# Start offsets of split weight buffers, modulo 256 bytes, in a two-layer decoder trunk

## The chip, the cores and the metric

The kernel runs on one core of a Trainium2 chip. The metric is the device time of one execution in microseconds (us). The engines are named as in the profile: PE is TensorE, with PEld its weight load, DVE is VectorE, ACT is ScalarE, POOL is GpSimd and SP is SyncE.

## The reference

Two layers over 256 tokens of width 1024, in float32. Cut to what matters here, which is the matrix products:

```python
for l in range(2):
    h = rms_norm(x, norm_mix_pre[l])
    q, k, v, lru_x, lru_gate, glu_in, gate_logits = split(h @ w_in[l])      # 1024 x 11776
    y_a = dilated_attention(q, k, v) @ w_o_attn[l]                          # 512 x 1024
    y_b = rg_lru(lru_x, lru_gate, lru_wa, lru_wx, ...) @ w_o_lru[l]         # 1024 x 1024
    y_c = conformer_conv(glu_in, ...) @ w_o_conv[l]                         # 1024 x 1024
    merged = sum_i sigmoid(gate_logits_i) * y_i
    x = x + rms_norm(merged @ w_out[l], norm_mix_post[l])                   # 1024 x 1024
    h = rms_norm(x, norm_mlp_pre[l])
    u = square(relu(h @ w_mlp_up[l]))                                       # 1024 x 4096
    x = x + rms_norm(u @ w_mlp_down[l], norm_mlp_post[l])                   # 4096 x 1024
```

## The kernel before

The host cuts all weights of a layer into 92 chunks of 128 partitions x 2048 float32 (1 MB each) and puts them in the order in which they are used (`chunk_plan`, `ORDER`). The kernel streams them in that order. The function `weights` does for one chunk: a DMA on SP into one of two `raw` buffers; a cast on ACT (line 416, in halves of 1024) that writes the high part `whi` in type float32r; a subtraction on DVE (line 429) that writes the low part `wlo`, which is raw minus high. The activations are split in the same way (`hh` and `hl`, `uh` and `ul`, and so on), and a product is three matmuls on PE (line 476): high by high, low by high, high by low.

There are two kinds of chunk.

- A **stationary** chunk (kinds `ws`, `rope` and `oa` in the plan: all of lx, lg, glu, q, k, ga, gb, gc, oa, ob, oc, and up but its first two chunks, which are ua). The weights are loaded into the array, 128 columns at a time, and 256 columns of activations stream past. `ws_items` sets the order of its 48 matmuls: two halves, and in each half first 16 matmuls with the high part (for each of 8 slices: with `hh`, then with `hl`), then 8 matmuls with the low part. In the trace such a half is 16 rows `whi_...` and one row `wlo_... x8`.
- A **moving** chunk (kind `as`: v, wo, ua and dn). Here the activations are loaded and 512 columns of weights stream past, 24 matmuls in one chunk. `as_items` sets the order: in each of two groups of 12, high and low part in turn for eight matmuls, then four with the high part.

All matmuls with weights follow each other on PE in the order of the plan (`main` chains them); a list scheduler with a cost model (`Sched.run`), which knows nothing of addresses, sets the rest. In the attention part (from the chunk q11 of a layer to its gc3) PE also does scores (`sc`), transposes (`tp`) and products with values (`pv`), which stand between the matmuls of the chunks, at the ends of the 16-row pieces above all. In the MLP each pair of up chunks is followed by a pair of dn chunks.

The addresses are what this case is about. `whi` and `wlo` have three buffers each (`NHI`), and the chunks take them in turn. A buffer has 2048 + 32 float32, which is 8320 bytes a partition, or 32 and a half times 256. So neighbouring buffers differ by 128 bytes modulo 256. In the built program the high buffers start at 128, 0 and 128 bytes modulo 256, the low buffers at 0, 128 and 0. Inside a buffer, a class `Shifted` begins the data 64 bytes (16 float32) late for stationary chunks and for v1 and v2, and at 0 for the other moving chunks. Data therefore stand like this, where "192/64" says that the high part begins 192 bytes and the low part 64 bytes past a multiple of 256:

| chunk | two chunks of three | every third chunk |
|---|---|---|
| stationary, and v1, v2 | 192/64 | 64/192 |
| v0, wo, ua, dn | 128/0 | 0/128 |

All slices inside a chunk are multiples of 256 bytes, so every matmul of a chunk has the offset of its part. The activations of the matmuls (`hh`, `hl`, `uh`, `ul`, the slots) all start 128 bytes past a multiple of 256. One chunk is an exception: the second dn chunk of the seventh group in layer 0 (`dn61`, "held") is split into eight slots, and there both parts stand at 128/128; its matmuls for the first 128 tokens and those for the second 128 tokens are run at two places.

The chunks of the MLP by their standing, in the order of time in layer 0: up4, up5 at 192/64; up6 at 192/64, up7 at 64/192; up8 at 64/192, up9 at 192/64; up10, up11 at 192/64, and so on with this period of three pairs. The dn pairs between them stand at 0/128 then 128/0; both at 128/0; 128/0 then 0/128; and so on.

Of the kernel before, what the change touches and what calls it, by code (L numbers as in the profile page):

```python
# [8 lines left out]
F32R = mybir.dt.float32r  # L9
# [4 lines left out]
P = 128  # L14
# [5 lines left out]
CHUNK = 2048  # L20
# [26 lines left out]
def chunk_plan():  # L47
    q0, k0, v0, lx0, lg0, gl0, br0 = 0, 1536, 3072, 4608, 5632, 6656, 8704
    plan = []

    def ws(name, mat, c0, c1=None):
        plan.append((name, "ws", mat, (c0, c0 + P if c1 is None else c1)))

    for n in ORDER:
        kind, a = n[:2], n[2:]
        if n[0] == "v":
            for kb in range(2):
                plan.append((f"{n}{kb}", "as", "w_in", (kb, v0 + int(n[1]) * 512)))
        elif n[0] in "qk":
            plan.append((n, "rope", "w_in", (q0 if n[0] == "q" else k0) + int(n[1]) * 512 + int(n[2]) * 256))  # L60
        elif kind == "gl":
            ws(n, "w_in", gl0 + int(n[3]) * P, gl0 + D + int(n[3]) * P)
        elif kind == "oa":
            plan.append((n, "oa", "w_o_attn", int(a) * 512))
        elif kind != "lw":
            mat, c0 = {"lx": ("w_in", lx0), "lg": ("w_in", lg0), "ga": ("w_in", br0), "gb": ("w_in", br0 + D),
                       "gc": ("w_in", br0 + 2 * D), "ob": ("w_o_lru", 0), "oc": ("w_o_conv", 0)}[kind]
            ws(n, mat, c0 + int(a) * 256)
    for c in range(2):
        for kb in range(2):  # L70
            plan.append((f"wo{c}{kb}", "as", "w_out", (kb, c * 512)))
    for kb in range(9):
        if kb == 0:
            plan += [(f"ua{k}", "as", "w_mlp_up", (k, 0)) for k in range(2)]
        elif kb < 8:
            ws(f"up{2 * kb}", "w_mlp_up", (2 * kb) * 256)
            ws(f"up{2 * kb + 1}", "w_mlp_up", (2 * kb + 1) * 256)
        if kb > 0:
            for c in range(2):
                plan.append((f"dn{kb - 1}{c}", "as", "w_mlp_down", (kb - 1, c * 512)))  # L80
    return plan
# [11 lines left out]
NHI = 3  # L93
# [10 lines left out]
LINE = 128  # L104
# [272 lines left out]
def trunk_kernel(ctx: ExitStack, tc: tile.TileContext, x_d, pos_d, w_d, lruw_d, par_d, gain_d, const_d, id_d, out_d):  # L377
    nc = tc.nc
    cp = ctx.enter_context(tc.tile_pool(name="cp", bufs=1))
    wp = ctx.enter_context(tc.tile_pool(name="wp", bufs=1))  # L380
    sp = ctx.enter_context(tc.tile_pool(name="sp", bufs=1))
    pp = ctx.enter_context(tc.tile_pool(name="pp", bufs=1, space=bass.MemoryType.PSUM))
    S = Sched()
# [4 lines left out]
    def slot(name, dt=F32, shape=(P, 2, T)):  # L388
        return S.buf(sp, shape, dt, "s2", name, NSLOT)
# [58 lines left out]
    def dma(eng, out, in_, nbytes):  # L448
        def fn():
            o = out.ap() if isinstance(out, View) else out  # L450
            i = in_.ap() if isinstance(in_, View) else in_
            eng.dma_start(out=o, in_=i)

        e = {id(nc.gpsimd): "POOL", id(nc.scalar): "ACT"}.get(id(eng), "SP")
        o = S.op(e, DMA_ISSUE[e], fn, views(in_), views(out))
        o.dma = nbytes / DMA_RATE / 1e3
        return o
# [40 lines left out]
    def split(hi, lo, src, scale=None):  # L498
        if scale is None:
            return act(hi, src, AF.Copy), tt(lo, src, hi.f32(), OP.subtract)  # L500
        return (act(hi, src, AF.Copy, scale=scale),
                stt(lo, src, scale, hi.f32(), OP.mult, OP.subtract))

    KIND = {p[0]: p[1] for p in chunk_plan()}
# [3 lines left out]
    def weights(l, name, spread=False):  # L508
        c = CIDX[name]
        assert c == used[l], (name, c, used[l])  # L510
        used[l] += 1
        nm = f"{name}_{l}"
        raw = S.buf(wp, (P, CHUNK), F32, "raw", f"raw_{nm}", NRAW)
        if l or c:
            o = dma(nc.sync, raw.all(), w_d[l * NCH + c], CHUNK * P * 4)
            if l == 0 and c in late:
                S.follow(o, late[c])
        else:
            for s in range(2):
                o = dma(nc.sync, raw[:, s * HALF:(s + 1) * HALF], w_d[0][:, s * HALF:(s + 1) * HALF], HALF * P * 4)  # L520
                if ORDER[0][0] == "v":
                    S.follow(o, x1_load)
        if spread:
            hs, ls = [], []
            for q in range(4):
                hs.append(slot(f"whi_{nm}{q}", F32R, (P, 512)))
                ls.append(slot(f"wlo_{nm}{q}", F32R, (P, 512)))
                for o in split(hs[q].all(), ls[q].all(), raw[:, q * 512:(q + 1) * 512]):
                    o.prep = True
            return [(Quarters(hs[2 * s:2 * s + 2]), Quarters(ls[2 * s:2 * s + 2])) for s in range(2)]  # L530
        off = 0 if KIND[name] == "as" and name[:2] not in ("v1", "v2") else LINE // 8
        hi = Shifted(S.buf(wp, (P, CHUNK + LINE // 4), F32R, "whi", f"whi_{nm}", NHI), off)
        lo = Shifted(S.buf(wp, (P, CHUNK + LINE // 4), F32R, "wlo", f"wlo_{nm}", NHI), off)
        n = HALF if l == 0 and c < 2 else PREP
        for b in range(0, CHUNK, n):
            for o in split(hi[:, b:b + n], lo[:, b:b + n], raw[:, b:b + n]):
                o.prep = True
        return [(Part(hi, s * HALF), Part(lo, s * HALF)) for s in range(2)]
# [201 lines left out]
    for l in range(L):  # L740
# [49 lines left out]
        def glu(i):  # L790
            w = weights(l, f"glu{i}")
            ps = mm_ps(f"glu{i}_{l}")
            gemm(f"glu{i}", w, ps, hr)
            if i % 2 == 0:
                upad[i // 2] = S.buf(sp, (P, 2, 288), F32, "upad", f"upad{i}_{l}", 4)
                memset(upad[i // 2][:, :, 0:30], 0.0)
            u2 = upad[i // 2]
            th = slot(f"gth{i}_{l}", shape=(P, T))
            act(th.all(), ps[:, 1, :], AF.Tanh, scale=0.5)
            stt(u2[:, i % 2, 30:30 + T], th.all(), 1.0, ps[:, 0, :], OP.add, OP.mult)  # L800
            if i % 2 == 1:
                conv_pair(i // 2)
# [3 lines left out]
        def lx(j):  # L806
            w = weights(l, f"lx{j}")
            ps = mm_ps(f"lx{j}_{l}")
            gemm(f"lx{j}", w, ps, hr)
            xp = S.buf(sp, (P, 2, 260), F32, "xp", f"xp{j}_{l}", 2)  # L810
            memset(xp[:, :, 0:3], 0.0)
            act(xp[:, :, 3:3 + T], ps.all(), AF.Copy)
            u = slot(f"lu{j}_{l}")
            for s in range(2):
                i = 2 * j + s
                act(u[:, s, :], ps[:, s, :], AF.Identity, scale=p1(par, CW + 24 + i), bias=p1(par, CB + i))
            for k in range(3):
                for s in range(2):
                    i = 2 * j + s
                    stt(u[:, s, :], xp[:, s, k:k + T], p1(par, CW + k * 8 + i), u[:, s, :], OP.mult, OP.add)  # L820
            lu[j] = u
            luh[j] = slot(f"luh{j}_{l}", F32R)
            lul[j] = slot(f"lul{j}_{l}", F32R)
            split(luh[j].all(), lul[j].all(), u.all())
# [3 lines left out]
        def lg(j):  # L828
            w = weights(l, f"lg{j}")
            ps = mm_ps(f"lg{j}_{l}")  # L830
            gemm(f"lg{j}", w, ps, hr)
            q = slot(f"gq{j}_{l}")
            act(q.all(), ps.all(), AF.Square, scale=0.044715 ** 0.5)
            stt(q.all(), q.all(), 1.0, ps.all(), OP.add, OP.mult)
            act(q.all(), q.all(), AF.Tanh, scale=0.7978845608028654)
            g = slot(f"gel{j}_{l}")
            stt(g.all(), q.all(), 1.0, ps.all(), OP.add, OP.mult)
            gel[j] = g
# [319 lines left out]
        for t in range(2):  # L1158
            nm = f"pm{l}{t}"
# [82 lines left out]
        for t in range(2):  # L1242
            nm = f"pd{l}{t}"
# [100 lines left out]
```

## Time and profile before

| | |
|---|---|
| median of 3 runs | 1123.68 us (1123.16 to 1127.1) |
| the profiled execution | 1124.8 us, of which its span is 1123.0 us |
| granted TensorE clock, mean | 0.998 |
| PE busy | 1103.7 us, 98% of the span |
| DVE busy | 903.7 us, 80% |
| ACT busy | 726.0 us, 65% |
| chain that ended last | PE 82%, DVE 9%, DMA 4%, ACT 3% |

The span is the time from the first to the last instruction. Busy times of matmuls overlap: a matmul of 256 columns is shown with 276 to 283 ns, while the next one starts 113 or 118 ns later. How fast PE really goes is therefore read from the starts of rows, or from the chain of work that ended last, where a piece of so many matmuls has a length without overlap.

### The profile page before, as it was taken

What the parts mean: (1) busy time and instruction counts of PE and PEld (TensorE: products, weight loads), DVE (VectorE), ACT (ScalarE), POOL (GpSimd) and SP (SyncE); (2) the same over time, 40 slices, a digit from 0 to 9 for tenths busy, and PEclk for the clock granted to TensorE, in tenths of its full rate; (3) what the DMA queues carried; (4) which work ended last, traced back from release to release, by engine and by line L of the source; (5) the groups of instructions that cost most, each with busy time, mean ns of one, the idle gap of its engine ahead of it and who ended that gap; (6) DMA issues with size and microseconds to landing.
All of it is one profiled execution on the core that took longest, in us unless ns stands there. A gap on an engine that the chain in (4) does not pass through costs nothing.

```text
span 1123.0 us, 20583 instructions
## 1 busy us (share of the span) xinstructions
PE 1103.7 (98%) x8258; PEld 1027.6 (92%) x8258; DVE 903.7 (80%) x1380; ACT 726.0 (65%) x1184; POOL 70.8 (6%) x156
## 2 busy tenths in 40 slices
PE   7999998999999999999999999999999999999997
PEld 6999998999999889988889999989989998988996
DVE  6999999999969875555679999999997789655554
ACT  5879938588765554444569897469766656444443
POOL 1000021111000010000000000221200001000000
PEclk9999999999999999999999999999999999999999
DMA  8654365655255555555556553765634365655551
GB/s 293 245 208 151 146 219 205 215 165 174 99 186 188 214 199 189 208 193 182 201 188 205 190 179 121 255 216 170 214 124 151 117 240 185 212 192 185 190 203 52
DMA packets 37649, 209.76 MB, mean 187 GB/s; under 512 B 6449, under 2 KB 9777, under 8 KB 14130
## 3 DMA queue, kind: packets, MB, share of 16 engines
q1 hardware_dynamic: 32976, 200.05, 50.7%
q0 software_dynamic: 4576, 8.40, 2.2%
q8 instruction: 65, 1.06, 0.4%
q14 instruction: 30, 0.25, 0.1%
q10 hardware_dynamic: 2, 0.00, 0.0%
HBM read 201.08 MB, written 1.05 MB: 180 GB/s over the span
## 4 chain that ended last, share of the span: by engine, by line
PE 82%; DVE 9%; DMA 4%; ACT 3%; issue 1%; SPq 1%; DVEq 0%; POOL 0%; ACTq 0%
PE dn L476 15%; PE up L476 14%; PE glu L476 8%; PE v L476 5%; PE gc L476 4%; PE wo L476 4%; PE lx L476 4%; PE oc L476 4%; PE lg L476 4%; PE k L476 3%; PE ga L476 3%; PE ob L476 2%; PE ua L476 2%; PE oa L476 2%; PE gb L476 1%; DMA qk<-r1q 1%
## 5 line engine op out<-in xcount | busy, mean ns | idle before, releaser
L429 DVE TENSOR_TENSOR wlo_dn<-raw_dn,whi_dn 128x1024 fp32r<-128x1024 f32 (+1 forms) x66 | 75.8, 1190 | 68.4 <-ACT whi_dn L416 68.4
L416 ACT CAST whi_dn<-raw_dn 128x1024 fp32r<-128x1024 f32 (+1 forms) x66 | 64.4, 1022 | 75.6 <-PE dn L476 44.0
L433 DVE SCALAR_TENSOR_TENSOR c<-upad,parh,c 128x256 f32<-128x256 f32 x256 | 110.5, 479 | 0.1
L476 PE MATMUL up<-hh_mlp,whi_up 128*128 128x256 f32 x448 | 106.3, 278 | 0.0
L476 PE MATMUL up<-hl_mlp,whi_up 128*128 128x256 f32 x448 | 106.0, 278 | 0.0
L476 PE MATMUL dn<-wlo_dn,uh 128*128 128x512 f32 x256 | 100.5, 393 | 0.0
L476 PE MATMUL dn<-whi_dn,uh 128*128 128x512 f32 x256 | 100.4, 392 | 0.0
L429 DVE TENSOR_TENSOR wlo_up<-raw_up,whi_up 128x1024 fp32r<-128x1024 f32 x56 | 66.4, 1222 | 39.1 <-ACT whi_up L416 39.1
L423 ACT ACTIVATE cpd<-upad,parh 128x256 f32<-128x256 f32 x224 | 94.6, 500 | 4.1 <-DVE c L429 4.1
L476 PEld LDWEIGHTS up<-hl_mlp,whi_up 128*128 128x128 f32 x448 | 84.3, 188 | 0.6
L476 PEld LDWEIGHTS up<-hh_mlp,whi_up 128*128 128x128 f32 x448 | 84.2, 188 | 0.6
L416 ACT CAST whi_up<-raw_up 128x1024 fp32r<-128x1024 f32 x56 | 56.2, 1048 | 36.4 <-PE dn L476 17.4
L476 PE MATMUL dn<-whi_dn,ul 128*128 128x512 f32 x256 | 70.8, 392 | 0.0
L429 DVE TENSOR_TENSOR cpd<-cpd 128x1024 f32<-128x1024 f32 (+2 forms) x84 | 63.5, 775 | 0.9 <-ACT cpd L423 0.9
L476 PE MATMUL up<-hh_mlp,wlo_up 128*128 128x256 f32 x448 | 60.7, 278 | 0.0
L476 PE MATMUL glu<-hl_mix,whi_glu 128*128 128x256 f32 x256 | 59.6, 276 | 0.0
L476 PE MATMUL glu<-hh_mix,whi_glu 128*128 128x256 f32 x256 | 59.6, 276 | 0.0
L476 PEld LDWEIGHTS dn<-whi_dn,ul 128*128 128x128 f32 x256 | 48.0, 188 | 10.8
L476 PEld LDWEIGHTS dn<-wlo_dn,uh 128*128 128x128 f32 x256 | 48.0, 188 | 10.3
L476 PEld LDWEIGHTS dn<-whi_dn,uh 128*128 128x128 f32 x256 | 48.1, 188 | 10.3
L476 PEld LDWEIGHTS up<-hh_mlp,wlo_up 128*128 128x128 f32 x448 | 55.7, 188 | 0.0
L476 PEld LDWEIGHTS glu<-hl_mix,whi_glu 128*128 128x128 f32 x256 | 48.0, 188 | 0.0
(309 smaller groups left out, 3388.3 us busy)
## 6 DMA issues: line engine op xcount, KB each, us to landing
raw_dn<-w_in_stream SPq DMA_DIRECT2D x32, 1024.0 KB, 4.8
raw_up<-w_in_stream SPq DMA_DIRECT2D x28, 1024.0 KB, 4.8
raw_glu<-w_in_stream SPq DMA_DIRECT2D x16, 1024.0 KB, 4.9
raw_q<-w_in_stream SPq DMA_DIRECT2D x12, 1024.0 KB, 4.8
raw_k<-w_in_stream SPq DMA_DIRECT2D x12, 1024.0 KB, 4.8
raw_v<-w_in_stream SPq DMA_DIRECT2D x11, 1024.0 KB, 4.9
raw_lx<-w_in_stream SPq DMA_DIRECT2D x8, 1024.0 KB, 4.8
raw_lg<-w_in_stream SPq DMA_DIRECT2D x8, 1024.0 KB, 4.8
```

The lines of the kernel that those rows point to most:

```text
L416: nc.scalar.copy(out.ap(), in_.ap())
L423: nc.scalar.activation(out.ap(), in_.ap(), func, scale=val(scale), **kw)
L429: lambda: nc.vector.tensor_tensor(out=out.ap(), in0=a.ap(), in1=b.ap(), op=op), [a, b], [out])
L433: lambda: nc.vector.scalar_tensor_tensor(out=out.ap(), in0=a.ap(), scalar=val(s), in1=b.ap(), op0=op0, op1=op1), [a, b] + views(s), [out])
L476: nc.tensor.matmul(out.ap(), lhsT=lhs.ap(), rhs=rhs.ap(), start=start, stop=stop)
```

## The change

The instructions of all five engines are the same before and after, in the same order; only addresses differ. A buffer gets 64 instead of 32 spare float32, so it has 8448 bytes, which is 33 times 256, and all six weight buffers of the built program start 128 bytes past a multiple of 256. The offset in the buffer becomes 192 bytes for the high and 64 bytes for the low part of stationary chunks, 192 bytes for both parts of v1 and v2, and stays 0 for the other moving chunks. What lies behind these buffers moves by 768 bytes, three times 256, and keeps its place modulo 256.

```diff
-        off = 0 if KIND[name] == "as" and name[:2] not in ("v1", "v2") else LINE // 8
-        hi = Shifted(S.buf(wp, (P, CHUNK + LINE // 4), F32R, "whi", f"whi_{nm}", NHI), off)
-        lo = Shifted(S.buf(wp, (P, CHUNK + LINE // 4), F32R, "wlo", f"wlo_{nm}", NHI), off)
+        offs = (3 * LINE // 8, LINE // 8) if KIND[name] != "as" else (3 * LINE // 8,) * 2 if name[:2] in ("v1", "v2") else (0, 0)
+        hi = Shifted(S.buf(wp, (P, CHUNK + LINE // 2), F32R, "whi", f"whi_{nm}", NHI), offs[0])
+        lo = Shifted(S.buf(wp, (P, CHUNK + LINE // 2), F32R, "wlo", f"wlo_{nm}", NHI), offs[1])
```

With the buffers' own start at 128, the data then stand like this:

| chunk | before | after |
|---|---|---|
| stationary | 192/64, every third 64/192 | 64/192 |
| v1, v2 | 192/64, every third 64/192 | 64/64 |
| v0, wo, ua, dn | 128/0, every third 0/128 | 128/128 |
| held dn61 | 128/128 | 128/128 |

## Rows read from the trace of the kernel before

**Rows 1.** The page: busy time, share, instructions; granted clock in 40 slices; chain.

```profile
PE 1103.7 (98%) x8258; PEld 1027.6 (92%) x8258; DVE 903.7 (80%) x1380; ACT 726.0 (65%) x1184; POOL 70.8 (6%) x156
PEclk9999999999999999999999999999999999999999
PE 82%; DVE 9%; DMA 4%; ACT 3%; issue 1%; SPq 1%; DVEq 0%; POOL 0%; ACTq 0%
```

**Rows 2.** Waits of PE: waiter <- waited for, total us, times, longest; first and last.

```profile
PE sc L476 <- DVE mx L969: 4.8, 2, 3.1
...
PE v L476 <- DVE hl_mix L429: 0.3, 1, 0.3
```

**Rows 3.** Chain of work that ended last: start us, length us, what (x matmuls).

```profile
30.41 27.20 PE glu L476 x240
...
363.53 20.73 PE wo L476 x90
...
421.47 11.31 PE up L476 x96
432.77 11.08 PE dn L476 x48
443.85 10.90 PE up L476 x96
454.75 11.01 PE dn L476 x48
465.76 11.08 PE up L476 x96
476.83 11.06 PE dn L476 x48
...
649.20 11.31 PE lg L476 x96
...
783.04 11.05 PE v L476 x48
...
1094.71 22.15 PE dn L476 x96
```

**Rows 4.** Timeline of PE, chunks up8, up9: start us, us, engine, line, matmuls merged.

```profile
467.48 1.11 PE L476 MATMUL up<-hh_mlp,wlo_up 128*128 128x256 f32 x8
...
470.30 1.09 PE L476 MATMUL up<-hh_mlp,wlo_up 128*128 128x256 f32 x8
...
473.04 1.07 PE L476 MATMUL up<-hh_mlp,wlo_up 128*128 128x256 f32 x8
...
475.76 1.07 PE L476 MATMUL up<-hh_mlp,wlo_up 128*128 128x256 f32 x8
```

**Rows 5.** Timeline of PE, the held chunk for the first tokens, then dn70.

```profile
548.62 0.39 PE L476 MATMUL dn<-whi_dn,uh 128*128 128x512 f32 x1
...
551.34 0.40 PE L476 MATMUL dn<-whi_dn,uh 128*128 128x512 f32 x1
...
554.11 0.39 PE L476 MATMUL dn<-whi_dn,uh 128*128 128x512 f32 x1
```

**Rows 6.** Timeline of PE, the held chunk for the other tokens, to its end.

```profile
556.87 0.39 PE L476 MATMUL dn<-whi_dn,uh 128*128 128x512 f32 x1
...
558.26 0.39 PE L476 MATMUL dn<-whi_dn,uh 128*128 128x512 f32 x1
...
559.62 0.40 PE L476 MATMUL dn<-whi_dn,uh 128*128 128x512 f32 x1
```

**Rows 7.** Timeline of PE, high part of ga0 and then ga2, layer 1.

```profile
822.17 0.28 PE L476 MATMUL ga<-hh_mix,whi_ga 128*128 128x256 f32 x1
...
823.94 0.28 PE L476 MATMUL ga<-hl_mix,whi_ga 128*128 128x256 f32 x1
...
832.87 0.28 PE L476 MATMUL ga<-hl_mix,whi_ga 128*128 128x256 f32 x1
...
834.46 0.28 PE L476 MATMUL ga<-hl_mix,whi_ga 128*128 128x256 f32 x1
```

## The prediction, made before the changed kernel was run

> **What bounds the kernel now.** I read the page first: PE is busy for 98% of the span, the chain that ended last is 82% PE, and PE has its full clock in all 40 slices [rows 1], so differences between matmuls are not differences of the clock. Then the waits of PE: the view has seven rows, together 12.7 us, the longest 4.8 us in total, and none is for a whi or wlo buffer [rows 2]. The splits on ACT and DVE, their DMAs and their order are thus covered. The time is set by the rate at which PE starts matmuls, and the question is whether that rate hangs on where the weights stand.
>
> The chain gives the rate, since its pieces don't overlap [rows 3]. Five glu chunks take 27.20 us for 240 matmuls, 113.3 ns each, and chunks of both standings are among them. In the MLP the pairs of up chunks, 96 matmuls each, take 11.31, 10.90 or 11.08 us: 117.8, 113.5 or 115.4 ns. So there is a fast rate of 113.3 and a slow one of 117.8, and the pairs repeat with the period of three in which the standing of the buffers repeats: 11.31 where both chunks stand at 192/64, 10.90 for 192/64 then 64/192, 11.08 for 64/192 then 192/64. The same three values come in both layers. The dn pairs, 48 matmuls, take 11.01 to 11.08 us, 229.4 to 230.8 ns.
>
> The timeline shows how a rate ends. In up8 (64/192) the first eight low matmuls take 1.11 us, the next eight 1.09, and in up9 they take 1.07 both times [rows 4]: up8 starts slow and becomes fast in its second low part, after some 40 matmuls, and up9 inherits the fast rate. I followed all stationary chunks so. Three regularities: a chunk that starts fast stays fast, at either standing, unless other work of PE comes between; a slow chunk at 192/64 stays slow to its end and hands that on (up4, up5; oa1 alone, whose slices lie with another step, does not); a slow chunk at 64/192 turns fast within its 48 matmuls, at its first or second low part, in every case without interruption but one (oa0). After a moving chunk, all eight chunks that stand at 64/192 start slow.
>
> Moving chunks have two such rates too. The held chunk, whose parts both stand at 128, takes 2.72 us for its 12 matmuls from 548.62 to 551.34, 226.7 ns each, while the next twelve, at 0/128, take 2.77 us, 230.8 [rows 5]. Its second group of 12 starts behind a slow chunk: six matmuls in 1.39 us (231.7), then six in 1.36 (226.7) [rows 6]. So with both parts alike the fast rate holds, and comes back after about six matmuls.
>
> **The change part by part.** No instruction is added, removed or moved. What changes is which standing each chunk has: all stationary chunks at 64/192, the moving ones at 128/128, v1 and v2 at 64/64. All of this lies on PE's path, so a saved nanosecond of rate is a saved nanosecond.
>
> *dn pairs.* At 226.7 ns a pair takes 10.88 us, and 0.03 more where it starts slow for six matmuls [rows 6]: 10.91. Twelve pairs now take 11.05 on average [rows 3], which saves 12 x 0.14 = 1.7. The last four chunks take 22.15 and would take 21.82: 0.3. Three chunks beside the held one in layer 0 save 0.2 together by the same price. Together 2.2 us. The bounds: 2.8 if every dn matmul is fast, and a loss of 0.2 if same standing doesn't carry over and all run at 231.7.
>
> *wo, ua, v0.* wo runs at 20.73 us for 90, 230.3 ns [rows 3]. Some 290 matmuls at 3.6 ns less are 1.0 us, but in half of them transposes come between and they start anew; I take 0.7 (0 to 1.2).
>
> *v1, v2.* They take 11.05 us for 48, 230.2 ns [rows 3]. No row shows both parts at 64. The nearest are the held chunk's 226.7 and 231.7 [rows 5, 6]: over 192 matmuls a gain of 0.7 or a loss of 0.3. I take half of the gain, 0.3, since alike they are but they stand elsewhere against the activations.
>
> *up.* With every dn pair ending fast at 128, up starts as up8 does, which also follows a fast dn chunk whose high part stands at 128: slow for 40 matmuls, then fast through the second chunk. Each pair takes 11.08. Twelve pairs take 132.96 us; now they take twice the sum of two rounds of 11.31, 10.90 and 11.08, about 133.1 [rows 3]. So 0.1 to 0.2 saved: the pairs of 11.31 gain what those of 10.90 lose. If the entry is fast instead, 12 x 0.2 = 2.4 more is saved; if no chunk recovers, 12 x 0.23 = 2.8 is lost.
>
> *Chunks without interruption elsewhere.* lg1 and lg2 of layer 1 take 11.31 us [rows 3]; at 64/192 the first would recover: 0.2. With the other lg chunks 0.3 (0 to 0.6). The long series of glu and oc keep the fast rate, since the fast rate has survived both standings and all seams that the new layout has: low at 192, then high at 64, is what happens in the middle of every 64/192 chunk now.
>
> *The attention part.* Here scores and transposes interrupt the chunks. The high part of ga0 (64) takes 1.77 us for 15 starts, 118 ns; that of ga2 (192) takes 1.59 for 14 starts, 113.6 [rows 7]. A slow high part of 16 costs 0.07 us, so 0.14 in a chunk; the low parts, now at 192, gain up to 0.07 of it back. Nineteen interrupted chunks at 192/64 get the other standing. Averaged over the starts of all thirty interrupted chunks, of which ga0 and ga2 are two, those at 64/192 lose 0.12 us against the fast rate and those at 192/64 0.07. The cost is 19 x 0.05 = 1.0 us (0 to 2).
>
> Sum: -2.2 - 0.7 - 0.3 - 0.15 - 0.3 + 1.0 = -2.65 us. The profiled execution, 1124.8 us, would become 1122.1. It is 1.1 above the median, so the median 1123.68 becomes 1121.0. All gains at their best give -7.8, all at their worst about +5.
>
> **A rule that speaks against all of this.** The terms above do without this paragraph. The Trainium skill, page "SBUF — State Buffer", section "Who interferes with whom", says that PE has two independent read ports, one for the moving operand and one for the weight load, and that "PE and ACT never wait on anyone". Its specifications give 16-byte cachelines, and 0, 64, 128 and 192 are all multiples of 16. By that, the offset is nothing and the time is 1123.7, the first rival. The trace disagrees as far as it goes: one instruction form runs at 113.3 and 117.8 ns at full clock [rows 1, 3].
>
> **The rivals.** First, nothing changes: the rates follow from what ran before, not from the address, and their period of three is that of the up and dn groups by chance. 1123.7. Against it: the period holds in both layers, where the buffers are shifted by one chunk. Second, faster: after dn at 128/128 the up chunks enter fast, and the attention part costs nothing. -2.65 - 2.4 - 1.0 - 0.2 is about -6.3: 1117.4. Against it: all eight entries after moving chunks at 64/192 are slow. Third, slower: the slow rate that 64 begins isn't ended by the low part, because what ended it in every third chunk was the change from a neighbour of the other standing, which is gone. oa0 of layer 0 stays slow through all its 48 matmuls at 64/192. Each chunk that stays slow costs 48 x 4.5 ns = 0.215 us. Some 80 chunks without interruption are fast now, 17 us in all, and the time would be up to 1138; slower than before from 13 such chunks on, and by over 0.5% from about 39.
>
> **How the numbers follow.** A measurement can tell about 0.5%, 5.6 us. Forecast: 57%, 1121.0, own range 1118.5 to 1124. Nothing changes: 16%. Faster: 17%. Slower, with many chunks slow: 10%, of which 3 stay within 0.5%. The range leaves out the far slow case and the best of the fast one: 1117 to 1125.5. Faster by over 0.5% 0.17, within 0.76, slower 0.07.
>
> **What the profile after would show.** Right: dn pairs at 10.88 to 10.95 us in the chain, each like the other; up pairs all near 11.08 with no period of three; glu at 27.20; high parts of ga and gc at 1.77. Wrong: dn pairs still at 11.05 (standing isn't it); up pairs at 10.88 (the second rival) or 11.31, and glu above 27.3 (the third).

## The result, and the profile after the change

The changed kernel takes 1116.41 us (median of 4 runs, 1116.08 to 1117.16); the kernel before, timed beside it, takes 1123.91 us. The ratio is 0.9923, with a 95% interval of 0.9903 to 0.9944: 7.5 us less, where 2.65 less was forecast, and below the range of 1117 to 1125.5. (A job is a set of kernels whose executions were timed beside each other.) In a second job, below, the changed kernel took 1118.58 us, inside the range, with a ratio of 0.9953 (0.9933 to 0.9973), 5.4 us less. The profiled execution takes 1116.5 us, its span 1114.8.

The page of the changed kernel, busy times and instructions:

```profile
PE 1097.1 (98%) x8258; PEld 1025.0 (92%) x8258; DVE 903.4 (81%) x1380; ACT 725.7 (65%) x1184; POOL 70.2 (6%) x156
```

The instruction counts are those of [rows 1]. PE's busy time, which adds overlapping matmuls, fell by 6.6 us and that of its weight loads by 2.6; DVE, ACT and POOL stayed within 0.6. What changed is how fast PE goes.

The chain of work that ended last, changed kernel (start us, length us, what, matmuls), where [rows 3] has the pieces of before:

```profile
30.22 27.20 PE glu L476 x240
...
358.86 20.43 PE wo L476 x90
...
405.36 10.90 PE dn L476 x48
416.27 11.07 PE up L476 x96
427.34 10.90 PE dn L476 x48
438.25 11.08 PE up L476 x96
...
643.13 10.88 PE lg L476 x96
...
775.82 11.04 PE v L476 x48
...
875.28 11.30 PE oa L476 x96
...
1086.81 21.80 PE dn L476 x96
```

The period of three is gone. Every up pair takes 11.08 us, where before 11.31, 10.90 and 11.08 took turns; every dn pair takes 10.90 instead of 11.01 to 11.08; wo's 90 matmuls take 20.43 instead of 20.73; the pair of lg takes 10.88 instead of 11.31. One thing is new and bad: the pair oa of layer 1 now takes 11.30, slow to its end.

The start of each chunk in the two timelines, subtracted, gives the whole difference by kinds of chunks. The sum of these is the difference of the spans, 8.25 us:

| chunks | forecast, us | measured, us |
|---|---|---|
| dn | -2.2 | -2.31 |
| wo, ua and v0 | -0.7 | -0.95 (wo and ua -0.75) |
| v1, v2 | -0.3 | -0.29 |
| up | -0.15 | -0.03 |
| lg, glu, lx, oa, oc | -0.3 | -0.37 (lg -0.90, glu and lx +0.30, oa and oc +0.23) |
| q, k, gb, ob, ga, gc, but for q11 of layer 0 | +1.0 | -0.95 |
| q11 of layer 0 | none | -3.24 |
| start of the program | none | -0.10 |

Two rows miss, by 1.95 and 3.24 us. The second is a single place. PE's timeline there, before (start us, us, what; in brackets the idle time before it and what ended it):

```profile
179.04 1.82 PE L476 MATMUL sc<-qk 64*128 64x256 f32 x12 [3.15 <-DVE mx L969]
180.80 2.07 PE L476 MATMUL q<-hh_mix,wlo_q 128*128 128x256 f32 x8
```

And after:

```profile
177.02 1.18 PE L476 MATMUL sc<-qk 64*128 64x256 f32 x12 [1.55 <-DVE mx L969]
178.13 1.20 PE L476 MATMUL q<-hh_mix,wlo_q 128*128 128x256 f32 x8
```

Before, PE waits 3.15 us for `mx`, and then the same twelve scores take 1.82 us instead of 1.18 and the eight low matmuls 2.07 instead of 1.20. The windows of before say why (stretch in us; length; busy us and instructions of PE, PEld, DVE, ACT, POOL; granted clock; DMA share; GB/s):

```profile
178.00:180.00 2.00, 0.96 (x7) 0.97 (x9) 2.00 (x6) 2.00 (x4) 0.15 (x1) 0.84 0.86 348
180.00:182.00 2.00, 2.00 (x14) 1.78 (x12) 2.00 (x3) 2.00 (x5) 1.69 (x4) 0.50 0.54 196
182.00:184.00 2.00, 2.00 (x16) 2.00 (x15) 2.00 (x5) 2.00 (x6) 0.90 (x3) 0.81 0.67 112
```

Behind the wait the granted clock falls to 0.50, 1.2 GHz; the three stretches with 0.84, 0.50 and 0.81 make some 3.4 us of it (0.64, 2.0 and 0.76). After, it is 1.00 in all three stretches. The wait itself is shorter because DVE is earlier, and DVE is earlier, as far as the waits in the two traces tell, because a load is. For the buffer `raw_ob`, whose split stands ahead of `mx`, the trace gives (line, operation, count, ns, first and last start) before:

```profile
L452 SPq DMA_DIRECT2D raw_ob<-w_in_stream x2: 333/334/336, 166.5 to 182.3; - x2
...
DMA to landing us min/median/max: 6.6/6.6/6.6
```

and after:

```profile
L452 SPq DMA_DIRECT2D raw_ob<-w_in_stream x2: 333/335/337, 165.5 to 180.3; - x2
...
DMA to landing us min/median/max: 5.0/5.0/5.0
```

It starts 1.0 us earlier and takes 1.6 less, so that the cast on ACT starts at 170.7 instead of 173.1. Whether addresses have anything to do with that is what the first experiments ask.

### The profile page after: what moved, and what is told of

It is laid out like the page before. It is cut to its first block, busy times and chain, and to the rows that moved or that the text cites. A ratio compares the mean times of both kernels' runs of the same rounds, so it can differ in the third digit from the quotient of the medians.

```text
span 1114.8 us, 20583 instructions
## 1 busy us (share of the span) xinstructions
PE 1097.1 (98%) x8258; PEld 1025.0 (92%) x8258; DVE 903.4 (81%) x1380; ACT 725.7 (65%) x1184; POOL 70.2 (6%) x156
## 4 chain that ended last, share of the span: by engine, by line
PE 83%; DVE 7%; DMA 5%; ACT 3%; issue 1%; SPq 1%; DVEq 0%; POOL 0%; ACTq 0%; POOLq 0%
PE dn L476 15%; PE up L476 14%; PE glu L476 8%; PE v L476 6%; PE gc L476 4%; PE ga L476 4%; PE lx L476 4%; PE wo L476 4%; PE oc L476 4%; PE lg L476 4%; PE k L476 3%; PE oa L476 2%; PE ua L476 2%; PE ob L476 2%; DMA raw_gb<-w_in_stream 2%; DMA qk<-r1q 1%
## 5 line engine op out<-in xcount | busy, mean ns | idle before, releaser
L476 PEld LDWEIGHTS glu<-hh_mix,whi_glu 128*128 128x128 f32 x256 | 48.1, 188 | 0.0
```

The source lines that it names most:

```text
L476: nc.tensor.matmul(out.ap(), lhsT=lhs.ap(), rhs=rhs.ap(), start=start, stop=stop)
```

## The experiments

The theory: PE's rate depends on where the weights stand modulo 256 bytes, and the saving is the sum of the chunks' changed rates. The rivals: the buffers' size or absolute place matters; or the saving is the wait at q11, which comes and goes with the landing of a load.

In the diffs, a and b are the places modulo 256 at which the high and the low part begin, n the number of the chunk in its turn, and kind "v" stands for v1 and v2. All kernels but the unchanged one have the new buffer size; the diffs are against the changed kernel, whose rule is written as these three cases.

### The kernel before, once more

No edit.

> The kernel before, unchanged, for a second trace. Question: is the stop of PE ahead of the scores in q11 of layer 0 (3.15 us idle, then 3.4 us at half the granted clock, in the first trace) an accident of one execution? Theory 'regular': it stands again at about 174 us, q11 takes 11.6 us, and the time is 1123 to 1125. Theory 'accident': q11 takes about 8.4 us as after the change, and the profiled execution is some 3 us shorter than the first one. The pairs in the MLP are as before by both: up 11.31, 10.90, 11.08, dn 11.05.

Measured: ratio 1.0001 (0.9983 to 1.0018), 1122.91 us. In the chain the pieces of up, dn, wo and lg are those of [rows 3] within 0.01 us. One series differs: in layer 1 lx1 starts slow here, and with it glu takes 27.48 us instead of 27.20, until a chunk at 64/192 ends it. The chunk q11 of layer 0, however, is 2.05 us shorter than in the first trace, with the same addresses. Its two waits for `mx` and the clock of the same stretch as above:

```profile
PE sc L476 <- DVE mx L969: 3.4, 2, 2.7
...
180.00:182.00 2.00, 2.00 (x20) 2.00 (x19) 2.00 (x3) 2.00 (x6) 1.50 (x4) 1.00 0.47 135
```

A wait of 2.7 us and no fall of the clock. So the rates are, but for such a start, which comes out differently at the same addresses, a property of the kernel, and a good part of the stop at q11 is one of the execution. That such stops vary fits the spread of this kernel's own times, 1120.8 to 1130.7 us in this job.

### New buffers, old standing

```diff
-    a, b = (128, 128) if kind == "as" else (64, 64) if kind == "v" else (64, 192)
+    if kind == "as": a, b = (0, 128) if n % 3 == 2 else (128, 0)
+    else: a, b = (64, 192) if n % 3 == 2 else (192, 64)
```

> The buffers of the change (8448 bytes, all alike), but each chunk's offsets are chosen so that it stands modulo 256 as before the change. Theory 'standing': only the place modulo 256 counts, so the time is that of before, 1123.9 (ratio 1.000, within 0.002), with up pairs of 11.31, 10.90, 11.08 us and dn pairs of 11.05. Theory 'place': the distance or size of the buffers counts, so it stays at 1116.4 (ratio 0.993).

Measured: 1.0005 (0.999 to 1.002), 1124.61 us. All addresses are those of the changed kernel to within 128 bytes, and the pieces of up, dn, wo, oa and oc are the old ones, to 0.01 us; lg is 0.22 us longer, by a slow start in layer 0. Chain of this kernel:

```profile
421.42 11.31 PE up L476 x96
432.73 11.07 PE dn L476 x48
443.80 10.89 PE up L476 x96
```

The interval leaves out the changed kernel's 0.9953, so the size and the absolute place of the buffers are not the cause. At q11 the wait was 2.3 us, and the clock fell, to 0.51 in the stretch of 180 to 182 us.

### The moving chunks alone, the stationary chunks alone

The first has the changed rule for v0, wo, ua and dn, and the old one for all others:

```diff
-    a, b = (128, 128) if kind == "as" else (64, 64) if kind == "v" else (64, 192)
+    if kind == "as": a, b = 128, 128
+    else: a, b = (64, 192) if n % 3 == 2 else (192, 64)
```

> Only v0, wo, ua and dn get the new standing (128/128); stationary chunks and v1, v2 stand modulo 256 as before. Theory 'terms': dn, wo, ua and v0 save 3.3 us together as in the trace after (dn pairs 10.90), the stationary chunks follow their old standings, with up pairs of 11.31 where both stand at 192/64, 11.08 or less elsewhere; ratio 0.997 if the stop in q11 stays, 0.994 if it goes. Theory 'stop': the stop goes with the time at which the work ahead of it runs, so it can go here as well; q11 8.4 instead of 11.6 us says so.

The second has the changed rule for the stationary chunks alone:

```diff
-    a, b = (128, 128) if kind == "as" else (64, 64) if kind == "v" else (64, 192)
+    if kind == "as": a, b = (0, 128) if n % 3 == 2 else (128, 0)
+    elif kind == "v": a, b = (64, 192) if n % 3 == 2 else (192, 64)
+    else: a, b = 64, 192
```

> Only the stationary chunks get the new standing (64/192); moving chunks and v1, v2 stand as before. Theory 'terms': dn pairs 11.05 as before, up pairs all about 11.08, lg and the attention part gain as after (0.9 and 1.0 us); ratio 0.998 if the stop in q11 stays, 0.9955 if it goes. If e2 and e3 together give less or more than the whole change (0.9923), the entry of one kind into the other counts: a dn pair of old standing may end so that up starts fast or slow.

Measured: the moving chunks alone 0.9996 (0.9982 to 1.001), 1122.17 us; the stationary chunks alone 0.9968 (0.995 to 0.9987), 1120.33 us. The chunks tell more than the totals. With the moving chunks alone dn gains 2.16 us and wo and ua 0.77, but up loses 1.23, which the expectation had not priced: a 192/64 chunk behind a fast dn chunk starts slow and stays so. Its chain:

```profile
407.95 10.90 PE dn L476 x48
418.86 11.31 PE up L476 x96
430.17 10.94 PE dn L476 x48
441.11 11.17 PE up L476 x96
```

With the stationary chunks alone up gains 1.33 us and lg 0.71, dn 0.07, and wo and ua nothing. Its up pairs do not all take the expected 11.08 us: 10.95, 10.88 and 11.08 take turns, with the standing of the dn pair ahead of them. Behind a dn pair at 0/128 then 128/0 the up pair is fast from its first matmul:

```profile
432.30 11.07 PE dn L476 x48
443.37 10.88 PE up L476 x96
```

In up the halves add up, to within 0.07 us: +1.23 and -1.33 make -0.10, and both together give -0.03. The new standing of the moving chunks costs up 1.2 to 1.3 us, with the old standing of up as with the new, because the rate at which a chunk starts is handed on by the chunk ahead of it, and the fast dn chunks hand on the worse start. More than half of what dn gains is lost so. The place q11 of layer 0, with no change of its stationary standing in the first of these kernels, is 2.20 us shorter than in the first trace of before, and 2.91 in the second.

### The changed kernel, once more

No edit.

> The changed kernel again, with more executions, beside moving_alone (0.9996) and stationary_alone (0.9968). Theory 'sum of rates': what both traces show in matmul rates (dn -2.3, wo and ua -0.75, v -0.5, lg -0.9, attention about -0.5 to -1.0, up 0) makes -5 to -5.5 us, ratio 0.995 to 0.9955. Theory 'rates and stop': the stop ahead of the scores in q11 of layer 0 is shorter with the new standing in every execution, -7.5 us, ratio 0.993. q11 of layer 0 in the trace: 8.4 us again, or 9 to 11 as in the three traces with old stationary standing.

Measured: 0.9953 (0.9933 to 0.9973), 1118.58 us against 1123.98. The kinds of chunks in the table above repeat within 0.07 us, but for v0 (0.4 us apart), for the start of the program (-0.47 against -0.10), for q11 (-3.98 against -3.24) and for q, k, gb and ob without it, which come to +0.66 here and to -0.69 there. PE's waits for `mx` in this trace:

```profile
PE sc L476 <- DVE mx L969: 2.4, 2, 1.7
```

So the part that the standing explains repeats: dn, wo, ua, v1, v2, up, lg, glu, lx, oa, oc, ga and gc save 4.0 us together in the first trace and 4.1 in this one. The rest of the difference moves from trace to trace. That the whole gain is one of stops of the clock can be ruled out: in this job the two executions of the changed kernel with a mean granted clock of 0.999 took 1117.1 and 1118.3 us, and the six of the kernel before with the same clock 1121.4 to 1125.6, 1123.7 in the mean.

### The mirror, and both parts alike

Three kernels differ from the changed one in the stationary chunks only. All at 192/64:

```diff
-    a, b = (128, 128) if kind == "as" else (64, 64) if kind == "v" else (64, 192)
+    a, b = (128, 128) if kind == "as" else (64, 64) if kind == "v" else (192, 64)
```

> As after the change, but all stationary chunks stand at 192/64 instead of 64/192. Theory 'which side': a slow chunk at 192/64 stays slow to its end and hands that on, and moving_alone has shown that up at 192/64 starts slow behind a fast dn. So every chunk from the entry to the end of its series is slow: up pairs 11.31 us, and the series lx, glu behind v0 5.65 us a chunk instead of 5.44; some 60 to 80 chunks at 0.215 us more than after, 13 to 17 us, 1129 to 1134 us, ratio 1.005 to 1.009. Theory 'alike is enough': that all buffers stand alike is what counts, not the side; 1116 to 1118, ratio 0.993 to 0.995.

All at 192/192:

```diff
-    a, b = (128, 128) if kind == "as" else (64, 64) if kind == "v" else (64, 192)
+    a, b = (128, 128) if kind == "as" else (64, 64) if kind == "v" else (192, 192)
```

> As after the change, but high and low part of stationary chunks both at 192. Theory 'step': what turns a slow series fast is the step of the weights from 64 to 192 between high and low part; without a step a series that starts slow stays slow, up pairs 11.31, ratio 1.003 or more. Theory 'alike': as with the moving chunks, parts that stand alike run fast by themselves after some matmuls: up pairs 10.88 to 10.95, and a time below the change, ratio 0.989 to 0.992.

All at 64/64:

```diff
-    a, b = (128, 128) if kind == "as" else (64, 64) if kind == "v" else (64, 192)
+    a, b = (128, 128) if kind == "as" else (64, 64) if kind == "v" else (64, 64)
```

> As after the change, but both parts of stationary chunks at 64. After the change a high part at 64 starts slow behind a moving chunk and behind most interruptions. Theory 'step': without the step to 192 it stays slow, up pairs 11.31, series behind v0 slow too, ratio 1.003 or more. Theory 'alike': fast after some matmuls, up pairs 10.88 to 10.95, ratio 0.989 to 0.992. If 64/64 and 192/192 differ, the distance to the activations (which start at 128) decides, not the step.

Measured: 1.0021 (1.0007 to 1.0034), 1126.58 us; 1.0026 (1.0013 to 1.0039), 1126.69; 1.0044 (1.0026 to 1.0061), 1128.36. The chain of the mirror:

```profile
30.46 28.27 PE glu L476 x240
...
421.07 11.31 PE up L476 x96
```

The long series glu, 27.20 us in the changed kernel, takes 28.27, which is 117.8 ns a matmul: lx1 starts slow behind v, nothing brings the fast rate back, and the slow one is handed on through all eleven chunks behind it. 192/192 and 64/64 give the same 28.27 and pairs of 11.31 and 11.30. So that both parts stand alike does not bring a slow stationary chunk back; of these four standings only the step inside the chunk from a high part at 64 to a low part at 192 does, and not the step back. It does not always: the pair oa of layer 1, whose slices lie with another step, stays slow at 64/192. The mirror is 8.0 us slower than the changed kernel of the same job, so the direction of the step is worth more than the whole change. It is less than the 1129 to 1134 us expected, since chunks that start fast stay so at 192/64 as well, as all of oa and oc do.

### Later scores

If the wait at q11 were the cause, moving what waits should show it. The second block of scores is put behind all of q11, in the old and in the new standing:

```diff
+        S.follow(starts["q11z"], score_ops[1])
```

where `q11z` is the last matmul of q11, kept beside its first:

```diff
+            starts[name + "z"] = S.ops[-1]
```

The old standing:

> The second scores of a layer, which PE waits for in the middle of q11 (3.15 us in the first trace of before, 2.7 and 2.3 in two more with that standing, 1.55 after), are put behind all of q11; DVE and ACT follow with their own order. Standing modulo 256 as before. Theory 'stop': with the wait gone q11 takes about 6.8 us, as in mirror and 192_192 where PE came late enough, and the time is 2 to 4 us below before, ratio 0.9965 to 0.998, if the new place costs nothing elsewhere. Theory 'the wait moves': DVE has the same work, so PE waits as long at the new place; ratio 1.000.

The new standing:

> The same, with the standing of the change (64/192, 128/128, 64/64). Set against late_old this is the change without the wait in q11. Theory 'sum of rates': 5.0 us below late_old (dn 2.3, lg 0.9, wo and ua 0.75, v 0.5, attention 0.4 and less), whatever late_old gives. Theory 'stop': if most of the 7.5 us were the wait, the difference is 2.5 to 3.5 us.

Measured: old 1.0015 (0.9996 to 1.0034), 1125.37 us; new 0.9975 (0.996 to 0.9991), 1121.28. The wait did not go, it moved. PE's waits, old standing:

```profile
PE ob L476 <- ACT thgb L423: 5.7, 2, 3.8
```

and new:

```profile
PE ob L476 <- ACT thgb L423: 5.0, 2, 3.1
```

The granted clock falls behind it in both (0.50 from 186 to 188 us), and once more in layer 1 in both. With the stops in both kernels, the new standing is still 4.1 us faster by the medians of one job, and 5.1 by the two traces. That is nearer to the 5.0 us of the rates than to the 2.5 to 3.5 of the stop, but the two intervals allow some 2 to 7 us, so it does not decide between them.

### Other standings, in one execution

Pairs of up chunks and the chunks v1 and v2 get a standing each; all else is the changed kernel:

```diff
+    scan = {("up4", 0): (0, 0), ("up5", 0): (0, 0), ("up6", 0): (0, 128), ("up7", 0): (0, 128), ("up8", 0): (128, 0), ...
+    if (name, l) in scan: a, b = scan[name, l]
```

> The change, but each up pair from up4 on has another standing: in layer 0 0/0, 0/128, 128/0, 128/128, 128/192, 192/128, in layer 1 64/0, 0/64, 64/128, 128/64, 0/192, 192/0 for the pairs 4 to 14; v1 and v2 stand at 128/128 and 0/0 in layer 0, 192/192 and 128/0 in layer 1, each first chunk of the pair given so with its second. One look, read by the pairs in the chain. Theory 'step': of the stationary standings only those with a step of the kind from 64 to 192 recover, the others take 11.31 us a pair. Theory 'distance': a standing at some other distance from the activations (128) starts fast, and its pair takes 10.88. For v: alike at 128 runs at 226.7 ns as dn does, at the other places at 230.

Measured: 1124.78 us, one execution. The up pairs, in us:

| layer 0 | us | layer 1 | us |
|---|---|---|---|
| 0/0 | 11.53 | 64/0 | 11.37 |
| 0/128 | 11.45 | 0/64 | 11.39 |
| 128/0 | 11.44 | 64/128 | 11.23 |
| 128/128 | 11.51 | 128/64 | 11.30 |
| 128/192 | 11.43 | 0/192 | 11.27 |
| 192/128 | 11.37 | 192/0 | 11.16 |

One of them and its dn neighbour in the chain:

```profile
420.41 11.53 PE up L476 x96
431.93 10.93 PE dn L476 x48
```

Neither theory holds as it was put: no pair starts fast and takes 10.88, and the others do not all take 11.31. None comes below the 11.08 of 64/192, and 128/128, good for the dn chunks, is with 0/0 the worst for stationary ones: 11.53 us is 120 ns a matmul, slower than the slow rate. Inside the pairs the two parts can have rates of their own. In up9 of layer 1, at 64/128, the sixteen high matmuls at 64 take 1.81 us, 113 ns each, and the eight low ones at 128 behind them 0.96 us, 120 ns each:

```profile
1025.69 0.28 PE L476 MATMUL up<-hh_mlp,whi_up 128*128 128x256 f32 x1
...
1027.50 1.12 PE L476 MATMUL up<-hh_mlp,wlo_up 128*128 128x256 f32 x8
1028.46 0.40 PE L476 MATMUL dn<-whi_dn,uh 128*128 128x512 f32 x1
```

So a rate is not only inherited: in all seven pairs that have a part at 128 it runs at some 119 to 120 ns, and the step from 64 to 192 is not the only way to a fast part. The dn pairs between the up pairs stay at 10.90 to 10.94.

The expectation that v at 128/128 runs at 226.7 ns as dn does failed. In layer 0, where v1 stands so, the last twelve matmuls of v1 take 2.80 us up to the start of ga0, 233.3 ns each:

```profile
265.68 0.39 PE L476 MATMUL v<-whi_v,hh_mix 128*128 128x512 f32 x1
...
268.48 0.28 PE L476 MATMUL ga<-hh_mix,whi_ga 128*128 128x256 f32 x1
```

In layer 1, v2 at 128/0 takes 11.06 us for 48, and v1 at 192/192 takes 8.40 for 36, again 233.3 ns, against 11.04 and 8.28 at 64/64, 230.0 ns:

```profile
782.61 11.06 PE v L476 x48
810.07 8.40 PE v L476 x36
```

v1 and v2 are moving chunks like dn, but they load every second token of the activations (`slice(t, T, 2)`), where v0, wo, ua and dn load neighbouring ones. Whether this makes the difference was not tried.

### A fast start for up

In the kernel before, the pairs of 10.90 us began at 192/64 behind a dn chunk at 128/0. This kernel makes that neighbourhood everywhere, for the price of a slower second dn chunk:

```diff
-    a, b = (128, 128) if kind == "as" else (64, 64) if kind == "v" else (64, 192)
+    if kind == "as": a, b = (128, 0) if name[:2] == "dn" and name[-1] == "1" and name != "dn71" else (128, 128)
+    elif kind == "v": a, b = 64, 64
+    elif name[:2] == "up" and int(name[2:]) % 2 == 0: a, b = 192, 64
+    else: a, b = 64, 192
```

> The new standing, but with what made the pairs of 10.90 us in the kernel before: the second dn chunk of a pair at 128/0 (not the held one and not the last), the first up chunk of a pair at 192/64, the second at 64/192. Theory: the rate at which a chunk starts is set by its own standing together with the standing of the chunk it follows; 192/64 behind 128/0 starts fast, in all four places where the kernel before had it. Then all up pairs behind such a dn chunk take 10.90 us instead of 11.08, 0.18 less for each of 12, which is 2.2 us less; the slower second dn chunk costs about 24 matmuls x 4.1 ns = 0.1 us in each of 13, 1.3 us more, so dn pairs near 11.00; sum -0.9 us against the changed kernel, a ratio to the kernel before of about 0.993 to 0.995. Rival: the fast entry in the kernel before came from the whole sequence of three pairs, and with this standing the entry is slow like all entries in the changed kernel; the slow rate then lasts through the first up chunk and 40 matmuls of the second: up pairs about 11.28, 2.4 us more, and with dn 3.7 us more: a ratio of 0.997 to 0.999.

Measured: 0.9975 (0.996 to 0.9991), 1121.11 us. Its chain:

```profile
449.81 10.96 PE dn L476 x48
460.76 11.17 PE up L476 x96
```

Neither expectation holds. The start is slow, so the neighbour's standing alone doesn't set it; but the second chunk becomes fast at its first low part, after 16 matmuls, where the rival had 40. Both pairs are slower than in the changed kernel, up by 1.3 us in all and dn by 0.7. What the place in the kernel before had and this one has not is the first dn chunk at 0/128; with it the start is fast in all four such places of the kernel before, and in all four of the kernel with the stationary chunks alone. It is no gain, since there the dn pair of 11.07 us and the up pair of 10.88 make 21.95, and in the changed kernel 10.90 and 11.07 make 21.97. Of the kernels tried the changed one is the fastest by its medians, though its interval in the second job overlaps that of the stationary chunks alone. 193 to 195 ns at the head of each of its up pairs remain lost, and what would give them back without such a price is not known.

## Why the prediction was wrong

**What held.** That the offset modulo 256 sets the rate, which was the base of the forecast: the old standing in new buffers has the old rates, and other standings have other rates. Of the terms, dn (2.31 against 2.2), up (0.03 against 0.15) and wo with ua and v0 (0.95 against 0.7, 0.20 of it v0, which does not repeat) came out as worked. v1 and v2 (0.29 against 0.3) came out by luck: the term was half of the way to the 226.7 ns of chunks whose parts stand alike, and they run at 230.0 throughout; standing alike does nothing for them, as 233.3 ns at 128/128 and 192/192 shows. Each up pair stands at 11.08 with a slow first chunk, as worked out, to 0.01 us. The chunks without interruption came to -0.37 against -0.3, but by another way: lg gained 0.90, three times the term, because the whole of lg stays fast where before a slow rate was handed on through it in both layers; and lx, oa and oc lost 0.5. Two sums of the forecast were off without effect: if all dn matmuls ran at 231.7 ns the loss would be about 1.0 us, not 0.2 (a pair would take 11.12 instead of 11.05, twelve times, and the other chunks in proportion), and the 290 matmuls of wo and ua leave out the 96 of v0.

**The step that failed: the attention part.** It was priced at +1.0 us. In the first trace it came to -0.95, -0.26 of it in ga and gc and -0.69 in q, k, gb and ob; in the second to +0.33, -0.33 in ga and gc and +0.66 in the others, which differ in their waits. In ga and gc, where both traces agree, there is a gain and no loss. Where it went wrong is in the averages. The chunks at 64/192 lost 0.12 us each before, the others 0.07, and I took this for a price of their own standing. In part it was their predecessors' debt. The chain of before, layer 1, from ob2 (192/64) to ga1 (64/192):

```profile
765.39 2.83 PE ob L476 x24
768.23 1.11 PE sc L476 x12
769.33 1.14 PE ob L476 x8
770.48 1.89 PE ga L476 x16
...
772.80 2.83 PE ga L476 x24
```

The same work after, both chunks at 64/192:

```profile
758.59 2.74 PE ob L476 x24
761.33 1.11 PE sc L476 x12
762.43 1.12 PE ob L476 x8
763.55 1.82 PE ga L476 x16
...
765.81 2.74 PE ga L476 x24
```

The scores stand between the high and the low part. A low part at 64 goes on slow behind them and hands that on: ga1's sixteen high matmuls took 1.89 us. A low part at 192 is fast again within a few matmuls, and ga1, at the very same 64/192 as before, takes 1.82. In the kernel before a chunk at 64/192 always followed one at 192/64 or a moving one, never another at 64/192; a class that always stands behind the same neighbours can't be priced by its own mean. In part it was their places: in the two traces of the changed kernel, where all thirty interrupted chunks stand at 64/192, the eleven that stood so before lose some 98 and 89 ns each, the other nineteen 72 and 78. Over all thirty the loss against the fast rate is now 82 ns each, where it was 72 and 122 for the two standings, 90 in the mean: a gain of about 0.2 us, not a loss of 1.0. The trap has caught one more sentence: in the kernel before all eight chunks at 64/192 behind a moving chunk started slow, but none of them stood behind a dn pair at 0/128 then 128/0, and the four that do with the stationary chunks alone start fast.

**The step that was missing: q11.** The page's row of tenths for the granted clock [rows 1] shows a 9 where it is 0.90 or more, in slices of 28 us; 3.4 us at half clock don't show in it. The sentence that PE has its full clock in all 40 slices was read as more than it says. And the longest wait of [rows 2], 3.1 us, was taken only as proof that no weight buffer is waited for. It was followed by a fall of the clock that made the place cost over 3 us more than in the changed kernel's trace. Against the first trace of before this place is 2.05, 0.95 and 2.20 us shorter in three more traces with the old stationary standing, and 3.24, 3.98, 2.91, 4.06 and, in the scan, 0.82 us shorter in five with the new one. So it belonged into the range, as a term of 0 to -4 us that moves by over 2 us without an edit.

**What the two misses make together.** The forecast of -2.65 had -3.65 of gains in it. Without the wrong +1.0 it is close to the 4.0 us that repeat. The second job's 5.4 us and the 4.1 us of the pair with later scores are near this. In the two traces of the first job the other 4.2 us are q11 (3.24), q, k, gb and ob (0.69), v0 (0.20) and the start of the program (0.10). Why the changed kernel's median is 2.2 us lower in the first job, with the same 1124 us beside it, stays open: its four executions there have mean granted clocks of 0.998 to 1.0 and all lie between 1116.1 and 1117.2 us, so stops of the clock alone do not explain it. Whether the new standing makes the stop at q11 rarer is not settled either: four of the five traces with the new stationary standing lie below all of the old, but the scan has a wait of 2.3 us and a fall of the clock there like the old ones.

**The rival that came near by luck.** The second rival's 1117.4 us is the nearest to the first job's time, but its main step, up chunks that enter fast, did not come: all up pairs stand at 11.08.

**Of the signs listed,** dn pairs at 10.88 to 10.95, up pairs at 11.08 without a period, and glu at 27.20 all came. High parts of ga at 1.77 for 15 starts came only in part: ga0 takes 1.88 for 16 in layer 1, but 1.81 in layer 0.

**The rule that spoke against the change.** The rows show one instruction form at 113.3 and 117.8 ns when nothing but the offsets of the weights differs, with the granted clock at full. The Trainium skill, page "SBUF — State Buffer", section "Who interferes with whom", has PE waiting on no one. That speaks of one engine waiting for another, which no run here shows; what the measurement decides against is what the prediction drew from it, that the offset is nothing. In all runs the activations stay 128 bytes past a multiple of 256, so whether the weights' own place counts or their distance from the activations is not told apart, and no run shows what part of the memory makes the difference.

## What to carry to other kernels

Where PE is the bound and its matmuls show two rates at full clock, compare the rates with the weights' addresses modulo 256: a standing that lets a slow chunk recover (here 64 for the part read first and 192 for the part read second; 128 for both in the chunks dn, wo and ua, where 512 columns of weights stream, but not in v1 and v2) was worth some 0.4% of the time for no instruction, and the wrong ones cost 0.2 to 0.4%. Try it on each kind of chunk by itself. Such a rate has memory: follow each chunk from what it inherits to what it hands on, and don't price a class by its mean where its neighbours are always the same. Look also at what a gain does to the next chunk: the fast dn chunks gained 2.2 us and cost up 1.2. Before a forecast, list every wait of PE above 1 us with the granted clock of the 4 us behind it, from windows of 2 us, since the page's slices hide them.

## What the runs showed of the hardware

- PE's rate with weights in float32r and 256 columns: 113.3 or 117.8 ns a matmul by the weights' start modulo 256 and by what ran before, and 120 at 0/0 and 128/128. Weights moved by a multiple of 256 keep their rates (the old standing in new buffers, pieces of up and dn within 0.01 us).
- With 512 columns of weights: 226.7 ns at 128/128 in dn, but 233.3 in v1, which loads every second token; 230.0 in v1 and v2 at 64/64.
- With 256 columns the fast rate is in part a state. It survives 240 matmuls of glu at 64/192; at 192/64, 192/192 and 64/64 the slow one survives as long (28.27 us).
- A wait of PE need not be long for its clock to fall, and its length does not decide alone: behind 3.15 us and 2.3 us of idling the granted clock was 0.50 and 0.51, that is 1.2 GHz, and behind 2.7 us it stayed at 1.00 (the kernel before, once more). What else decides is not shown.
